# Feed-forward layers of a hybrid encoder: statistics inside the plain pair, a negation behind the last leading part, shared gate tiles, a third block begun early

## The chip, the cores and the metric

One NeuronCore of a Trainium2 chip runs the whole program as a single launch. The metric is the time of one execution on the device in microseconds; the number of a kernel is the median of its runs.

## What is computed

An encoder of width 1024 over 512 tokens with two layers. Each layer is a feed-forward network (FFN), a mixer (attention of several kinds), a cross attention to 256 memory rows, and a second FFN. So there are four FFNs, called FFN0 to FFN3 here. The change touches the FFNs, and the normalisation of the memory rows, which is prepared while FFN0 runs.

```python
def rmsnorm(x, g):
    y = xf * lax.rsqrt(jnp.mean(xf * xf, axis=-1, keepdims=True) + EPS)
    return (y * g.astype(jnp.float32)).astype(x.dtype)
def swiglu(x, wg, wu, wd):
    return (jax.nn.silu(x @ wg) * (x @ wu)) @ wd
...
    h = x
    for layer in range(DEPTH):
        h = h + 0.5 * swiglu(rmsnorm(h, g), wg, wu, wd)      # g, wg: [1024], [1024, 2816]
        h = h + even_mixer(...)                              # odd_mixer in layer 1
        h = h + memory_xattn(rmsnorm(h, mg), rmsnorm(mem, sg), wq, wkv, qg, kg, wo)
        h = h + 0.5 * swiglu(rmsnorm(h, g), wg, wu, wd)
```

## The kernel before

Activations lie transposed in SBUF, features on the partitions, as eight tiles of 128 by 512 tokens. Every fp32 operand of a product is split into a leading part (`xh`, `wh`, `hh`, rounded by ScalarE) and a rest (`xl`, `wl`, `hl`, a subtraction on VectorE), and a product is three matmuls: leading by leading, leading by rest, rest by leading (`LEAD` is the first two, `REST` the third). TensorE is called PE, VectorE DVE, ScalarE ACT, GpSimd POOL and SyncE SP.

An FFN has 22 blocks of 128 hidden features, taken in pairs. The first pair (`plain_pair`) multiplies the whole x with both blocks of wg and wu in plain matmuls of 128x512 (L317). The other ten pairs use a scheme with seven instead of eight products on quarters: `open_pair` (product of w11), `sum_pair` (products with the token sums t1 and t2, the second weight operand of which is the pair's `sh`/`sl` or `wh`/`wl`), `cross_pair` (products of w12 and with t3) and `close_pair` (`lower`, with t4, and `upper`). All of these matmuls are line L432. Weights of the quarters are read by SP (`fetch`, L419), two of them are sums that POOL makes with an accumulating DMA (L462, L484, the latter after ACT's negation at L483). `operand` (L410 on ACT, L411 on DVE) splits them; every third operand has tiles of its own (`sh`, `sl`, one buffer), the others share two buffers.

The norm of the tokens is not applied to x before the product but to the result: the factor R, one number for each token spread over 128 partitions, multiplies the gate's argument and the down result. Its way is: squares of x summed into `acc`; PE transposes `acc` (`column_sums`, L249); DVE reduces (L251) and forms v (L258); POOL raises v to the power -0.5 (L242, r); PE transposes r into a PSUM bank (L329); DVE copies it to R (L331). DVE also forms the token sums t1 to t4 (`token_sums`, tiles tq, L368 to L384) at this place.

After the pairs 4, 8 and 10 a chunk of hidden features (8, 8 and 6 blocks) is multiplied down (`down`, L553; the sum into x is L563 and L564). `down` has eight output blocks d. It begins two of them early without the chunk's last two hidden blocks (`down_products` with tail False) and brings these in when the gate of the last pair has made them (`hidden_parts`, L355 on ACT and L356 on DVE). In the last chunk the first block is begun before the last pair is closed, and the gates of that pair (L514 to L518) are computed in two halves, one behind `upper` and one behind `lower`.

PE executes in the order in which the code issues matmuls. The queues of the other engines are filled by a scheduler that follows priorities (`tc.high_priority`) and a constraint called `behind` (`issue_after`), which keeps an instruction from being queued before another one. The eight tiles of memory rows are loaded and squared in `mem_stats`, which the program calls behind pair 2 of FFN0; its column sums on PE stand ahead of the t1 product of pair 3.

Of the kernel before, what the change touches and what calls it, by code (L numbers as in the profile page):

```python
# [11 lines left out]
F32 = mybir.dt.float32  # L12
F32R = mybir.dt.float32r
BF = mybir.dt.bfloat16
AF = mybir.ActivationFunctionType
# [89 lines left out]
class Encoder:  # L105
# [45 lines left out]
    def wfill(self, tiles, src, sl, eng, after=None):  # L151
        nc = self.nc
        w, wh, wl = tiles
        dma = self.loaded = nc.sync.dma_start(w[:, sl], src[:, sl])
        nc.scalar.activation(wh[:, sl], w[:, sl], AF.Copy)  # L155
        with self.behind(after):
            eng.tensor_sub(wl[:, sl], w[:, sl], wh.bitcast(F32)[:, sl])  # L157
        return dma
# [104 lines left out]
    def ffn(self, pre):  # L263


        with ExitStack() as ctx:
            pool = lambda name: ctx.enter_context(self.tc.tile_pool(name=pre + name, bufs=1))
            f = self.f = SimpleNamespace(pre=pre, hp=pool("h"), tp=pool("t"), H={}, n=0, last=None)
            R = self.plain_pair()
            ends = [sum(CHUNKS[:c + 1]) // 2 for c in range(len(CHUNKS))]  # L270
            c = 0
            pair = self.open_pair(1)
            R()
            for p in range(1, FB // 2):
                final = p == FB // 2 - 1
                self.sum_pair(pair)
                if p in ends:
                    self.down(c)
                    c += 1
                self.cross_pair(pair)  # L280
                if final:
                    early = self.block(c, 0, True)
                    self.down_products(c, early, LEAD, False)
                    self.close_pair(pair, True)
                    self.down(c, early)
                else:
                    old, pair = pair, self.open_pair(p + 1)
                    self.close_pair(old, False)
                if p == 2 and self.mem_r is None:
                    self.mem_stats()  # L290

    def plain_pair(self):
        nc, I, f = self.nc, self.I, self.f
        xs, order = self.xs, self.order
        self.wshare = 0
        banks = []
        for b in range(2):
            ws, self.ws = self.ws, None
            after = self.rest if b == 0 and self.chained else None
            ws = ws or [self.wload(I[f.pre + w][b], 1024, after) for w in ("wg", "wu")]  # L300
            pp = [self.bank("pa"), self.bank("pb" if b else "pa")]
            banks.append(pp)
            if b == 0:
                head = order[:KB // 2]
                groups = [(ks, ((0, 0), (0, 1))) for ks in (head, order[KB // 2:KB - 1], order[KB - 1:])]
                if self.mem_r is None:
                    groups[1:1] = [(head, ((1, 0),))]
                    groups.append((order[KB // 2:], ((1, 0),)))
                else:
                    groups.append((order, ((1, 0),)))  # L310
            else:
                groups = [(order, ((0, 0), (0, 1), (1, 0)))]
            for ks, ops in groups:
                for w, p in zip(ws, pp):
                    for a, c in ops:
                        for k in ks:
                            nc.tensor.matmul(p, w[a][:, k * P:(k + 1) * P], xs[k][c],  # L317
                                             start=k == order[0] and a == c == 0, stop=k == order[-1] and a == 1)
        f.after = self.loaded
        with self.behind(self.summed), self.behind(self.squared):  # L320
            self.token_sums()
        v, r = self.stats(self.acc, QB)
        return lambda: self.plain_end(banks, r)

    def plain_end(self, banks, r):
        nc, f = self.nc, self.f
        p = self.bank("pb")
        for i in range(QB):
            nc.tensor.transpose(p[:, i * P:(i + 1) * P], r[:, i:i + 1].to_broadcast([P, P]), self.ident)  # L329
        f.R = f.tp.tile([P, S], F32, name="R", tag="R", bufs=1)  # L330
        nc.vector.tensor_copy(f.R, p)  # L331
        gs = f.tp.tile([P, 1024], F32, name="gs", tag="gs")
        for b in range(2):
            nc.vector.tensor_mul(gs[:, b * S:(b + 1) * S], banks[b][0], f.R)
        self.hidden(0, gs, [pp[1] for pp in banks])
# [66 lines left out]
    def operand(self, t, own=None):  # L402

        nc, f = self.nc, self.f
        if own is None:
# [4 lines left out]
        nc.scalar.activation(h, t, AF.Copy)  # L410
        nc.vector.tensor_sub(l, t, h.bitcast(F32))  # L411
        return h, l

# [2 lines left out]

    def fetch(self, t, p, q):
        with self.behind(self.f.after):
            self.nc.sync.dma_start(t, self.quarter(p, q))  # L419
        return t  # L420

    def raw_quarter(self, p, q):
# [48 lines left out]
    def cross_pair(self, pair):  # L471
# [8 lines left out]
        with self.tc.high_priority():  # L480
            s = f.tp.tile([P, 1024], F32, name="s3", tag="s3", bufs=2)
            self.fetch(s, p, 2)
            nc.scalar.activation(s, s, AF.Copy, scale=-1.0)  # L483
            nc.gpsimd.dma_start(s, self.quarter(p, 0), accum_op=OP.add)  # L484
            w = self.operand(s)
        self.product(pair.y, w, f.B["3"], False)
# [4 lines left out]
    def close_pair(self, pair, final):  # L491
# [16 lines left out]

        gu = pair.gu.rearrange("p (b z t) -> p b z t", b=2, z=2)
        if final:  # L510
            for b, step in enumerate((upper, lower)):
                step()
                gs = f.tp.tile([P, 1024], F32, name="gs", tag="gs")[:, :S]
                nc.vector.tensor_mul(gs, gu[:, b, 0, :], f.R)  # L514
                t = f.tp.tile([P, 1024], F32, name="t", tag="t")[:, :S]
                nc.scalar.activation(t, gs, AF.Tanh, scale=0.5)
                nc.vector.scalar_tensor_tensor(t, t, 1.0, gs, op0=OP.add, op1=OP.mult)  # L517
                nc.vector.tensor_mul(gs, t, gu[:, b, 1, :])  # L518
                self.hidden_parts(p, gs, b)
            return  # L520
        lower()
        upper()
# [33 lines left out]
    def down(self, c, first=None):  # L556
# [9 lines left out]
                self.made(d, self.x[d])  # L566

        early = [first or self.block(c, 0), self.block(c, 1)]
        for b in early[first is not None:]:
            self.down_products(c, b, LEAD, False)  # L570
        for b in early:
            self.down_products(c, b, REST, False)
        for d, b in enumerate(early):
            self.down_products(c, b, LEAD + REST, True)
            done(d, b[1])
        for d in range(2, KB):
            b = self.block(c, d)
            self.down_products(c, b, LEAD + REST, False)
            self.down_products(c, b, LEAD + REST, True)
# [506 lines left out]
    def mem_stats(self):  # L1086
        nc = self.nc
        with ExitStack() as ctx:
            mp = ctx.enter_context(self.tc.tile_pool(name="ms", bufs=2))
            acc, powed = None, self.powed  # L1090
            for k in range(KB):
                m = mp.tile([P, NMEM], F32, name="mem", tag="mem", bufs=4)
                with self.behind(self.loaded):
                    nc.sync.dma_start(m, self.I["memT"][k * P:(k + 1) * P, :])
                with self.behind(powed):
                    acc = self.square(acc, m, NMEM, mp)
            v, r = self.stats(acc, 2)
            self.mem_r = self.const.tile([P, 2], F32, name="mem_r")
# [420 lines left out]
```

## Time and profile before

| | us |
|---|---|
| three runs | 2183.46, 2184.88, 2185.17 |
| median | 2184.88 |
| the profiled execution | 2184.71 |
| its span in the trace | 2182.9 |

| engine | busy us | share of the span |
|---|---|---|
| PE | 2105.0 | 96% |
| DVE | 1571.6 | 72% |
| ACT | 1138.4 | 52% |
| POOL | 361.1 | 17% |

PE is busy for 2105.0 of the span of 2182.9 us, so all its idle time together is 77.9 us. Its busy time is not the same at all places: behind a long idle time the same matmuls take longer, which the granted clock of a stretch tells (1.00 is the level of 2.4 GHz, 0.50 that of 1.2 GHz). An idle time is charged to the instruction that came last by the trace.

### The profile page before, as it was taken

The numbers are of one execution on the slowest core, as the hardware profiler recorded it, in microseconds if no ns is written. First come the engines' busy times: TensorE is split into PE (matmuls) and PEld (weight loads), VectorE is DVE, ScalarE is ACT, GpSimd is POOL, SyncE is SP. The second block draws the span as 40 slices with busy tenths as digits, with TensorE's granted clock in tenths as the row PEclk, the third lists the DMA queues.
The fourth block names the chain that finished last, engine by engine and source line by source line (L and its number), as shares of the span: only waits on it lengthen the run. The fifth ranks groups of instructions, "written<-read, shape, count | busy, mean of one in ns | idle before, by whom it ended". The sixth has DMA issues, their size and how long they took to land. (4 is left out here: it accounts for less than half of the span.)

```text
span 2182.9 us, 32518 instructions
## 1 busy us (share of the span) xinstructions
PE 2105.0 (96%) x12834; PEld 1881.6 (86%) x12834; DVE 1571.6 (72%) x2242; ACT 1138.4 (52%) x1701; POOL 361.1 (17%) x319
## 2 busy tenths in 40 slices
PE   6999999999999989999999999999999998999998
PEld 5989997887778879898979899988888877989996
DVE  6858677479876687585778677675668677858675
ACT  5525444465686565363555355344778565525442
POOL 2100002335432110000020000003453022000000
PEclk8999999999999999999999999999999999999999
DMA  7637533322142166474346456334223215636532
GB/s 225 165 116 187 151 102 118 138 73 77 66 134 69 66 174 174 119 190 127 95 145 176 125 165 176 102 104 159 79 86 126 97 59 154 170 110 185 155 100 82
DMA packets 86121, 279.65 MB, mean 128 GB/s; under 512 B 9680, under 2 KB 12880, under 8 KB 85968
## 3 DMA queue, kind: packets, MB, share of 16 engines
q1 hardware_dynamic: 74448, 235.62, 32.6%
q0 software_dynamic: 11520, 41.95, 10.8%
q8 instruction: 101, 1.65, 0.3%
q14 instruction: 52, 0.43, 0.1%
HBM read 271.24 MB, written 6.29 MB: 127 GB/s over the span
## 5 line engine op out<-in xcount | busy, mean ns | idle before, releaser
L155 ACT ACTIVATE wh<-wf 128x1024 fp32r<-128x1024 f32 (+2 forms) x211 | 215.4, 1022 | 357.5 <-PE ps_pa L553 124.7
L157 DVE TENSOR_TENSOR wl<-wf,wh 128x1024 fp32r<-128x1024 f32 (+2 forms) x169 | 201.3, 1194 | 49.1 <-ACT wh L155 47.9
L411 DVE TENSOR_TENSOR wl<-s,wh 128x1024 fp32r<-128x1024 f32 x108 | 132.1, 1223 | 70.6 <-ACT wh L410 70.6
L410 ACT ACTIVATE wh<-s 128x1024 fp32r<-128x1024 f32 x108 | 114.3, 1058 | 105.7 <-PE ps_pb L432 38.2
L410 ACT ACTIVATE wh<-wf 128x1024 fp32r<-128x1024 f32 x84 | 89.1, 1060 | 107.8 <-PE ps_pa L553 31.2
L157 POOL TENSOR_TENSOR wl<-wf,wh 128x1024 fp32r<-128x1024 f32 x42 | 102.4, 2438 | 141.1 <-ACT wh L155 139.5
L484 POOL DMA_DIRECT2D s<-l_ffn_wq x40 | 35.4, 884 | 532.7 <-ACT s L483 532.7
L653 PE MATMUL ps_pa<-wh,xh 128*128 128x512 f32 x384 | 123.1, 402 | 0.0
L653 PE MATMUL ps_pa<-wh,xl 128*128 128x512 f32 x384 | 119.8, 393 | 0.0
L653 PE MATMUL ps_pa<-wl,xh 128*128 128x512 f32 x384 | 119.1, 391 | 0.0
L462 POOL DMA_DIRECT2D s<-l_ffn_wq x40 | 35.5, 887 | 448.5 <-DMA s<-l_ffn_wq 356.8
L411 DVE TENSOR_TENSOR wl<-wf,wh 128x1024 fp32r<-128x1024 f32 x84 | 102.8, 1224 | 4.4 <-ACT wh L410 4.4
L563 DVE TENSOR_TENSOR dn<-ps_pa,R 128x512 f32<-128x512 f32 x48 | 33.1, 690 | 95.9 <-PE ps_pa L553 95.9
L553 PE MATMUL ps_pb<-hh,wh 128*128 128x512 f32 x352 | 97.2, 394 | 0.0
L553 PE MATMUL ps_pb<-hl,wh 128*128 128x512 f32 x352 | 96.7, 393 | 0.0
L553 PE MATMUL ps_pb<-hh,wl 128*128 128x512 f32 x352 | 96.4, 392 | 0.0
L222 POOL TENSOR_TENSOR acc<-acc,sq 128x512 f32<-128x512 f32 (+1 forms) x37 | 46.6, 1260 | 268.1 <-ACT sq L221 267.1
L553 PE MATMUL ps_pa<-hh,wh 128*128 128x512 f32 x328 | 89.7, 392 | 0.0
L553 PE MATMUL ps_pa<-hh,wl 128*128 128x512 f32 x328 | 88.7, 389 | 0.0
L553 PE MATMUL ps_pa<-hl,wh 128*128 128x512 f32 x328 | 88.7, 389 | 0.0
L563 DVE TENSOR_TENSOR dn<-ps_pb,R 128x512 f32<-128x512 f32 x48 | 33.1, 689 | 76.2 <-PE ps_pb L553 76.2
L653 PEld LDWEIGHTS ps_pa<-wh,xl 128*128 128x128 f32 x384 | 72.6, 189 | 16.0
(376 smaller groups left out, 5997.3 us busy)
## 6 DMA issues: line engine op xcount, KB each, us to landing
wf<-l_ffn_wq SPq DMA_DIRECT2D x120, 512.0 KB, 3.3
s<-l_ffn_wq SPq DMA_DIRECT2D x80, 512.0 KB, 4.5
s<-l_ffn_wq POOLq DMA_DIRECT2D x80, 512.0 KB, 6.5
wf<-l_ffn_wd SPq DMA_DIRECT2D x64, 512.0 KB, 3.9
wf<-l_w_in SPq DMA_DIRECT2D x48, 512.0 KB, 3.2
wf<-l_ffn_wd SPq DMA_DIRECT2D x32, 384.0 KB, 3.1
wf<-l_mem_wkv SPq DMA_DIRECT2D x16, 512.0 KB, 3.3
wf<-l_w_out SPq DMA_DIRECT2D x16, 512.0 KB, 3.2
```

What stands on the lines that cost most here:

```text
L155: nc.scalar.activation(wh[:, sl], w[:, sl], AF.Copy)
L157: eng.tensor_sub(wl[:, sl], w[:, sl], wh.bitcast(F32)[:, sl])
L222: self.summed = (eng or nc.gpsimd).tensor_add(acc[:, :n], acc[:, :n], sq[:, :n])
L410: nc.scalar.activation(h, t, AF.Copy)
L411: nc.vector.tensor_sub(l, t, h.bitcast(F32))
L462: nc.gpsimd.dma_start(pair.s, self.quarter(p, 2), accum_op=OP.add)
L484: nc.gpsimd.dma_start(s, self.quarter(p, 0), accum_op=OP.add)
L553: self.nc.tensor.matmul(bank, w[a][:, j * P:(j + 1) * P], h, start=j == a == e == 0, stop=j == nb - 1 and (a, e) == ops[-1])
L563: nc.vector.tensor_mul(t, bank, f.R)
L653: nc.tensor.matmul(banks[i], xs[k][a][:, i * P:(i + 1) * P], w[b][:, kk * 512:kk * 512 + 512], start=k == a == b == 0, stop=k == KB - 1 an ...
```

## The change

It has five parts. (a) The transposes of `acc`, the reduction, v and r are issued inside the plain pair, behind the first product of its second block, at high priority, and the transposes of r with the copy to R follow right behind the plain pair, ahead of `open_pair(1)`. (b) The negation of ACT at the head of an FFN (L483) is queued behind the last leading part of the plain pair. (c) The two half gates of the last pair use the two halves of one `gs` and one `t` tile, and the parts of the first half are queued behind `lower`. (d) The first block of the last `down` does 12 instead of 8 matmuls ahead of `upper`, and a third block is begun early. (e) `fetch` records itself as the latest load, so that the loads and squares of the memory rows, which are queued behind the latest load and leading part, come later.

```diff
@@ wfill, operand, fetch
-        nc.scalar.activation(wh[:, sl], w[:, sl], AF.Copy)
+        self.leading = nc.scalar.activation(wh[:, sl], w[:, sl], AF.Copy)
...
-            self.nc.sync.dma_start(t, self.quarter(p, q))
+            self.loaded = self.nc.sync.dma_start(t, self.quarter(p, q))
@@ ffn, plain_pair
-            R = self.plain_pair()
+            self.plain_pair()
             pair = self.open_pair(1)
-            R()
...
+                    if b == 1 and p is pp[0]:
+                        with self.tc.high_priority():
+                            v, r = self.stats(self.acc, QB)
+        f.after, f.led = self.loaded, self.leading
...
-        v, r = self.stats(self.acc, QB)
-        return lambda: self.plain_end(banks, r)
         p = self.bank("pb")
         f.R = f.tp.tile([P, S], F32, name="R", tag="R", bufs=1)
-        nc.vector.tensor_copy(f.R, p)
+        with self.tc.high_priority():
+            for i in range(QB):
+                nc.tensor.transpose(p[:, i * P:(i + 1) * P], r[:, i:i + 1].to_broadcast([P, P]), self.ident)
+            nc.vector.tensor_copy(f.R, p)
@@ ffn, cross_pair
-                    self.down_products(c, early, LEAD, False)
+                    self.down_products(c, early, LEAD + REST, False)
...
-            nc.scalar.activation(s, s, AF.Copy, scale=-1.0)
+            with self.behind(f.led):
+                nc.scalar.activation(s, s, AF.Copy, scale=-1.0)
@@ close_pair
+            gs2 = f.tp.tile([P, 1024], F32, name="gs", tag="gs")
+            t2 = f.tp.tile([P, 1024], F32, name="t", tag="t")
+
+            def gate(b):
+                gs, t = (x[:, b * S:(b + 1) * S] for x in (gs2, t2))
                 nc.vector.tensor_mul(gs, gu[:, b, 0, :], f.R)
                 nc.scalar.activation(t, gs, AF.Tanh, scale=0.5)
                 nc.vector.scalar_tensor_tensor(t, t, 1.0, gs, op0=OP.add, op1=OP.mult)
                 nc.vector.tensor_mul(gs, t, gu[:, b, 1, :])
-                self.hidden_parts(p, gs, b)
+                return gs
+
+            upper()
+            with self.tc.high_priority():
+                gs = gate(0)
+            lower()
+            with self.tc.high_priority():
+                self.hidden_parts(p, gs, 0)
+                self.hidden_parts(p, gate(1), 1)
@@ down
+        if first is not None:
+            early.append(self.block(c, 2))
+        fresh = early[first is not None:]
+        for ops in (LEAD, REST):
+            for b in fresh:
+                self.down_products(c, b, ops, False)
...
-        for d in range(2, KB):
+        for d in range(len(early), KB):
@@ mem_stats
-                with self.behind(self.loaded):
+                with self.behind(loaded):
...
-                with self.behind(powed):
+                with self.behind(powed), self.behind(leading):
                     acc = self.square(acc, m, NMEM, mp)
```

Three places of the queues show what moves. The first is DVE at the head of FFN3 before the change; `s` and v are the statistics, `sl` is the rest of the second operand of pair 1.

```order
L377 SCALAR_TENSOR_TENSOR t1l<-tq,t1h 128x1024
L368 SCALAR_TENSOR_TENSOR tq<-x,cols,tq 128x256 x2
L375 TENSOR_TENSOR t3l<-tq,t3h 128x1024
L411 TENSOR_TENSOR wl<-wf,wh 128x1024
L375 TENSOR_TENSOR t2l<-tq,t2h 128x1024
L411 TENSOR_TENSOR wl<-s_17848,wh 128x1024
L251 TENSOR_REDUCE s<-ps_pb 128x4
L375 TENSOR_TENSOR t4l<-tq,t4h 128x1024
L466 TENSOR_TENSOR s_17848<-s_17848,wf 128x1024
L411 TENSOR_TENSOR wl<-wf,wh 128x1024
L258 TENSOR_SCALAR v<-s 128x4
L411 TENSOR_TENSOR sl<-s_17848,sh 128x1024
```

The same place of the same queue after the change, from the reduction on; lines have other numbers there (L366 is L368 of before, L375 is L377, L373 is L375, L409 is L411, L329 is L331).

```order
L251 TENSOR_REDUCE s<-ps_pb 128x4
L366 SCALAR_TENSOR_TENSOR tq<-x,cols,tq 128x256
L375 SCALAR_TENSOR_TENSOR t1l<-tq,t1h 128x1024
L366 SCALAR_TENSOR_TENSOR tq<-x,cols,tq 128x256 x2
L373 TENSOR_TENSOR t3l<-tq,t3h 128x1024
L258 TENSOR_SCALAR v<-s 128x4
L409 TENSOR_TENSOR wl<-wf,wh 128x1024
L373 TENSOR_TENSOR t2l<-tq,t2h 128x1024
L409 TENSOR_TENSOR wl<-s_17842,wh 128x1024
L373 TENSOR_TENSOR t4l<-tq,t4h 128x1024
L329 COPY R<-ps_pb 128x512
L464 TENSOR_TENSOR s_17842<-s_17842,wf 128x1024
```

The reduction has moved from behind five large operations to ahead of them, and v from behind eight to behind two; the copy to R now stands ahead of the operations that make `sl`, and behind these rows come `wl`, the two `gs` multiplications and then `sl`.

The second place is POOL in FFN0 before the change; `acc` are the sums of the memory squares, L462 and L484 the accumulating DMAs.

```order
L242 TENSOR_TENSOR r<-v,mhalf 128x4
L222 TENSOR_TENSOR acc<-acc,sq 128x256 x7
L484 DMA s_1009<-l_ffn_wq 128x1024
L462 DMA s_916<-l_ffn_wq 128x1024
L484 DMA s_1513<-l_ffn_wq 128x1024
L462 DMA s_1148<-l_ffn_wq 128x1024
L242 TENSOR_TENSOR r<-v,mhalf 128x2
```

And after the change (L483 and L460 are the accumulating DMAs there):

```order
L242 TENSOR_TENSOR r<-v,mhalf 128x4
L483 DMA s_1009<-l_ffn_wq 128x1024
L460 DMA s_916<-l_ffn_wq 128x1024
L483 DMA s_1513<-l_ffn_wq 128x1024
L222 TENSOR_TENSOR acc<-acc,sq 128x256 x6
L460 DMA s_1148<-l_ffn_wq 128x1024
L222 TENSOR_TENSOR acc<-acc,sq 128x256
L242 TENSOR_TENSOR r<-v,mhalf 128x2
```

The memory sums have moved behind three DMAs, and the last of them behind the DMA of `s_1148`, which belongs to pair 4. On ACT, in the same stretch, the negation of `s_489` now stands behind the last `wh` of the plain pair, and no memory square stands ahead of `t1h`; before, three did.

The third place is DVE at the last pair of FFN3, before the change, from the first half gate on.

```order
L514 TENSOR_TENSOR gs<-gu,R 128x512
L157 TENSOR_TENSOR wl<-wf,wh 128x768
L517 SCALAR_TENSOR_TENSOR t<-t,gs 128x512
L518 TENSOR_TENSOR gs<-t,gu 128x512
L356 TENSOR_TENSOR hl<-gs,hh 128x512
L514 TENSOR_TENSOR gs<-gu,R 128x512
L517 SCALAR_TENSOR_TENSOR t<-t,gs 128x512
L518 TENSOR_TENSOR gs<-t,gu 128x512
L356 TENSOR_TENSOR hl<-gs,hh 128x512
```

And after it:

```order
L515 TENSOR_TENSOR gs<-gu,R 128x512
L157 TENSOR_TENSOR wl<-wf,wh 128x768
L517 SCALAR_TENSOR_TENSOR t<-t,gs 128x512
L515 TENSOR_TENSOR gs<-gu,R 128x512
L518 TENSOR_TENSOR gs<-t,gu 128x512
L517 SCALAR_TENSOR_TENSOR t<-t,gs 128x512
L354 TENSOR_TENSOR hl<-gs,hh 128x512
L518 TENSOR_TENSOR gs<-t,gu 128x512
L354 TENSOR_TENSOR hl<-gs,hh 128x512
```

The first multiplication of the second gate has moved ahead of the last two operations of the first, and the two gates run interleaved.

## Rows read from the trace of the kernel before

**Rows 1.** What PE waited for: engine, line, releaser: us in total, times, longest

```profile
PE ps_pb L329 <- POOL r L242: 25.6, 4, 12.5
PE ps_pa L553 <- ACT hh L355: 14.9, 4, 3.7
PE ps_pb L432 <- DVE gu L489: 3.0, 4, 0.7
```

**Rows 2.** Timeline of PE at R in FFN0, FFN2, FFN3: start, us, [idle before]

```profile
48.80 1.11 PE L329 MATMUL ps_pb<-ident,r 128*128 128x128 f32 x4 [12.52 <-POOL r L242]
...
1152.70 0.65 PE L329 MATMUL ps_pb<-ident,r 128*128 128x128 f32 x4 [1.01 <-POOL r L242]
...
1850.25 1.11 PE L329 MATMUL ps_pb<-ident,r 128*128 128x128 f32 x4 [6.04 <-POOL r L242]
```

**Rows 3.** Timeline of PE in FFN3: first open product, t1, t2 by `sl`

```profile
1841.10 0.72 PE L432 MATMUL ps_pa<-xh,wh 128*128 128x256 f32 x4
...
1856.02 0.64 PE L432 MATMUL ps_pa<-t2h,sl 128*128 128x256 f32 x4
```

**Rows 4.** Timeline of DVE at the head of FFN3

```profile
1837.53 1.22 DVE L377 SCALAR_TENSOR_TENSOR t1l<-tq,t1h 128x1024 fp32r<-128x1024 f32 x1
...
1839.46 1.22 DVE L375 TENSOR_TENSOR t3l<-tq,t3h 128x1024 fp32r<-128x1024 f32 x1
...
1844.00 0.68 DVE L251 TENSOR_REDUCE s<-ps_pb 128x4 f32<-128x512 f32 x1
...
1848.08 1.22 DVE L411 TENSOR_TENSOR sl<-s,sh 128x1024 fp32r<-128x1024 f32 x1
...
1852.13 1.29 DVE L334 TENSOR_TENSOR gs<-ps_pa,R 128x512 f32<-128x512 f32 x2
```

**Rows 5.** Windows at r, FFN3, FFN2: PE PEld DVE ACT POOL busy, PEclk, DMA share

```profile
1848.20:1850.30 2.10, 0.05 (x1) 0.05 (x1) 2.07 (x2) 0.00 (x0) 1.95 (x1) 0.50 0.72 250
1151.60:1152.70 1.10, 0.09 (x1) 0.00 (x1) 0.36 (x1) 1.10 (x2) 1.04 (x1) 1.00 0.14 34
```

**Rows 6.** Timeline of FFN0: plain pair, memory square, t1h, t2 by `sl`

```profile
21.78 2.12 PE L317 MATMUL ps_pa<-xh,wh 128*128 128x512 f32 x8 [1.85 <-ACT wh L155]
...
35.41 0.42 ACT L221 ACTIVATE sq<-mem 128x256 f32<-128x256 f32 x1 [2.51 <-DMA mem<-memT]
35.73 1.04 ACT L372 ACTIVATE t1h<-tq 128x1024 fp32r<-128x1024 f32 x1
...
55.73 0.64 PE L432 MATMUL ps_pa<-t2h,sl 128*128 128x256 f32 x4
```

**Rows 7.** Timeline near the memory sums: SP's fetch, POOL's DMA, PE

```profile
85.83 0.33 SPq L419 DMA_DIRECT2D s<-l_ffn_wq  x1
...
91.14 0.86 POOL L462 DMA_DIRECT2D s<-l_ffn_wq  x1 [7.51 <-DMA s<-l_ffn_wq]
...
92.21 0.38 PE L249 MATMUL ps_pb<-ident,acc 128*128 128x128 f32 x2
```

**Rows 8.** Timeline of the end of FFN3: PE, ACT and DVE

```profile
2134.96 0.74 PE L432 MATMUL ps_pb<-xh,wh 128*128 128x256 f32 x4 [0.74 <-DVE gu L489]
...
2140.81 1.09 PE L553 MATMUL ps_pb<-hh,wh 128*128 128x512 f32 x4
...
2141.80 0.57 ACT L499 COPY gu<-ps_pa 128x512 f32<-128x512 f32 x1
...
2144.46 0.45 PE L553 MATMUL ps_pa<-hh,sh 128*128 128x512 f32 x1
...
2145.12 0.69 DVE L514 TENSOR_TENSOR gs<-gu,R 128x512 f32<-128x512 f32 x1
...
2148.64 0.80 PE L553 MATMUL ps_pa<-hh,sh 128*128 128x512 f32 x1 [3.73 <-ACT hh L355]
```

**Rows 9.** Windows behind that wait, first and last of the four FFNs

```profile
349.10:351.80 2.70, 2.70 (x8) 2.04 (x7) 0.83 (x2) 0.00 (x0) 0.00 (x0) 0.53 0.00 0
...
2149.20:2154.00 4.80, 4.80 (x13) 3.67 (x12) 1.75 (x4) 0.84 (x1) 0.00 (x0) 0.51 0.11 44
```

More of the change, by code (lines that the diff above doesn't have):

```diff
@@ L318, in plain_pair @@
                                              start=k == order[0] and a == c == 0, stop=k == order[-1] and a == 1)
-        f.after = self.loaded
+                    if b == 1 and p is pp[0]:
+                        with self.tc.high_priority():
+                            v, r = self.stats(self.acc, QB)
+        f.after, f.led = self.loaded, self.leading
         with self.behind(self.summed), self.behind(self.squared):
             self.token_sums()
-        v, r = self.stats(self.acc, QB)
-        return lambda: self.plain_end(banks, r)
-    def plain_end(self, banks, r):
-        nc, f = self.nc, self.f
         p = self.bank("pb")
-        for i in range(QB):
-            nc.tensor.transpose(p[:, i * P:(i + 1) * P], r[:, i:i + 1].to_broadcast([P, P]), self.ident)
         f.R = f.tp.tile([P, S], F32, name="R", tag="R", bufs=1)
-        nc.vector.tensor_copy(f.R, p)
+        with self.tc.high_priority():
+            for i in range(QB):
+                nc.tensor.transpose(p[:, i * P:(i + 1) * P], r[:, i:i + 1].to_broadcast([P, P]), self.ident)
+            nc.vector.tensor_copy(f.R, p)
         gs = f.tp.tile([P, 1024], F32, name="gs", tag="gs")
@@ L409, in operand @@
                 for n in (("sh", "sl") if own else ("wh", "wl"))]
-        nc.scalar.activation(h, t, AF.Copy)
+        self.leading = nc.scalar.activation(h, t, AF.Copy)
         nc.vector.tensor_sub(l, t, h.bitcast(F32))
@@ L510, in close_pair @@
         if final:
-            for b, step in enumerate((upper, lower)):
-                step()
-                gs = f.tp.tile([P, 1024], F32, name="gs", tag="gs")[:, :S]
+            gs2 = f.tp.tile([P, 1024], F32, name="gs", tag="gs")
+            t2 = f.tp.tile([P, 1024], F32, name="t", tag="t")
+            def gate(b):
+                gs, t = (x[:, b * S:(b + 1) * S] for x in (gs2, t2))
                 nc.vector.tensor_mul(gs, gu[:, b, 0, :], f.R)
-                t = f.tp.tile([P, 1024], F32, name="t", tag="t")[:, :S]
                 nc.scalar.activation(t, gs, AF.Tanh, scale=0.5)
@@ L568, in down @@
         early = [first or self.block(c, 0), self.block(c, 1)]
[L569 to L572, printed above, removed]
+        if first is not None:
[4 more added lines that the diff above has]
+                self.down_products(c, b, ops, False)
         for d, b in enumerate(early):
@@ L1089, in mem_stats @@
             mp = ctx.enter_context(self.tc.tile_pool(name="ms", bufs=2))
-            acc, powed = None, self.powed
+            acc, loaded, leading, powed = None, self.loaded, self.leading, self.powed
             for k in range(KB):
                 m = mp.tile([P, NMEM], F32, name="mem", tag="mem", bufs=4)
-                with self.behind(self.loaded):
+                with self.behind(loaded):
                     nc.sync.dma_start(m, self.I["memT"][k * P:(k + 1) * P, :])
-                with self.behind(powed):
+                with self.behind(powed), self.behind(leading):
                     acc = self.square(acc, m, NMEM, mp)
```

## The prediction

> **What bounds the kernel now.** The first thing to read is the list of engines, as in the table above: PE is busy for 2105.0 of 2182.9 us, so nothing that another engine does is worth anything unless PE waits for it, and all its idle time is 77.9 us. The second view is the list of what PE waited for [rows 1]. Three of its groups lie where the change works: 25.6 us before the transposes of r, once in each FFN, 14.9 us at the ends of the FFNs for `hh` of the last pair's second gate, and 3.0 us for the bank into which `upper` goes on. The timeline splits the first group into 12.52 us in FFN0, 1.01 in FFN2 and 6.04 in FFN3 [rows 2], which leaves 6.03 for FFN1. FFN0 has one more, 1.85 us, where PE waits for a `wh` that stands behind ACT's negation [rows 6]. That is 45.4 us of stalls. The third view is the granted clock: behind the 3.73-us stall at an FFN's end PE works 2.70 us at 0.53 in the first FFN and 4.80 us at 0.51 in the last, so 1.3 and 2.4 us are lost there [rows 9], 1.8 on average. With as much behind the longer stalls at three heads, some 58 us is all that can be won.
>
> **The ends of the FFNs (parts c and d).** In FFN3 `upper` starts at 2134.96 after 0.74 us of waiting, and the down block behind `lower` at 2140.81 [rows 8]. Between the two lie 48 matmuls that don't change. From 2140.81 PE does 16 down matmuls and begins the tail's first at 2144.46 [rows 8]: 3.65 us, 0.228 each. Four matmuls more in the first block are 0.91 us; they fill the 0.74, and the block behind `lower` starts at about 2141.0. There PE now has two fresh blocks, 24 matmuls or 5.5 us, where it had 12 and the four that moved: it comes to the tail at 2146.5 and to its second matmul at 2146.7.
>
> That one waits for the second gate, which before begins at 2145.12, although its `gu` was copied by 2141.80 + 0.57 = 2142.4 [rows 8]: DVE was still in the first gate, whose `hl` stands ahead of it. From 2145.12 to 2148.64 are 3.52 us, five steps of 0.70. With tiles of its own the second gate begins ahead of the first one's last multiplication, at about 2143.0, and the two run interleaved: on DVE `gs`, the first gate's `gs`, t, `hl` and `gs`, 0.69 each, with tanh beside them, and then `hh` on ACT, 0.63 by the same pitch. That is 4.1 us: 2147.1. So a stall of some 0.4 us stays, and PE is 1.54 us earlier with 12 matmuls (2.74 us) more done: 4.3 us for one FFN and 17.1 for four, whose stalls are alike (14.9 us in 4, the longest 3.7 [rows 1]). Behind the stall of 0.74 the clock did not fall (48 matmuls in the 5.85 us from 2134.96 to 2140.81 is 0.12 for one of 256 columns, as fast as 0.228 for 512), so behind 0.4 it should not either, and 1.8 us come back in each of four: 7.2. Sum for the ends 24.3. Bounds: if the gates did not interleave at all, 2148.64 would stay and only the 12 matmuls count, 11 us for four; nothing above 24.3 and four times 0.4, or 26. I take 24.3, because each step has a row.
>
> **The heads of FFN1 and FFN3 (part a).** In FFN3 the reduction runs at 1844.00, though PE was past its transposes by 1841.10 [rows 3], since DVE works through the token sums first [rows 4]. Its new place is ahead of `t1l`, which started at 1837.53; the reduction takes 0.68, so `t1l` moves to 1838.2, `t3l` follows after the same 1.93 us, and behind its 1.22 comes v at 1841.3. r takes 1.95 us beside a full DVE [rows 5]: 1843.4. PE, done with the plain pair by 1841.10, waits some 2.4 us instead of 6.04. Here the gain is not the stall that goes, since `sl` is late next. From `t3l` at 1839.46 to `sl` at 1848.08 DVE did seven large operations, the reduction and v (0.7 together) [rows 4], so a large one takes 1.14. Behind v now stand `wl`, t2l, `wl`, t4l (4.6), the copy to R (0.65, as one of the two `gs` [rows 4]), the subtraction and `wl` (2.3), two `gs` (1.3) and `sl` (1.2): 1851.4. PE starts the first matmuls with `sl` at 1856.02 before [rows 3]. After the change it has ahead of them the transposes (0.8), the open product (1841.10 to 1850.25 less 6.04, which is 3.1), the product with t1 (as much) and 0.96 of t2: from 1843.4 to about 1851. It waits up to 0.9 us for `sl` and goes on at 1851.4 to 1851.9. So 4.1 to 4.6 us are gained; I take 4.4 here and the same for FFN1, whose stall is the same: 8.8. Bounds for each: 0, if `sl` comes no sooner, and 7, the stall and a clock lost behind it.
>
> **The head of FFN2 (part a).** Its wait of 1.01 us [rows 2] goes: 1.0, between 0 and 1.
>
> **The head of FFN0 (parts a, b and e).** The negation goes behind the `wh` of the plain pair, and 1.85 us go. The three memory squares ahead of `t1h` go too: the last of them waited 2.51 us for its load and ran at 35.41, `t1h` at 35.73 [rows 6]. Without them `t1h` follows its sums, by my reading some 6 us sooner, v behind `t3l` comes at 34 to 35, and r two us later. PE arrives at 48.80 - 12.52 - 1.85 - 2.9 (the open product, now behind it), that is at 31.5, and waits about 5 us. The DVE steps of above then give `sl` at 44 to 46, where PE used it at 55.73 [rows 6]: 10 to 11.7 us. I take 10, since the operands of this head wait for loads as well. Bounds: 6 (the 1.85 and the 6 us of `t1h`, less two of clock), and 13.
>
> **The memory sums (part e): a new wait.** PE did them at 92.21 without waiting [rows 7]. Now their last addition on POOL stands behind the accumulating DMA of pair 4, which POOL issued only at 91.14, as it had waited for SP's fetch of 85.83 to land. PE and the fetch both move up by the 10 of above. In the times of before that DMA is issued by 92.0, and behind it come one addition (0.9, a row like the DMA's 0.86) and a semaphore or a late load, against PE at 92.2: between 0 and 5 us, of which I take 2.2. Queued on PE behind it is all of pair 3, whose operands have that time to get ready.
>
> An operation of POOL can be longer than its own work: r took 1.95 us where DVE was busy for 2.07 of 2.10 us, and 1.04 where it was busy for 0.36 of 1.10 [rows 5]. By the rows the addition is 0.9 us late at the worst, within my 2.2. The Trainium skill (SBUF — State Buffer, "Who interferes with whom") says that the only contention is an exclusive lock on the port pair that VectorE and GpSimd share, so the loser stands still until the other's instruction ends. The 0.9 us agree with its direction. By that rule the addition may wait for a whole operation of DVE, 1.22 us [rows 4], and the total would be 2144.0 instead of the sum below.
>
> **The sum.** 24.3 + 8.8 + 1.0 + 10 - 2.2 = 41.9 us. The profiled execution took 2184.71 us, 0.17 under the median, so the forecast is 2142.8 us.
>
> **Rivals.**
> - **The heads give little.** `sl`, not R, is what PE needs; if the steps ahead of it on DVE wait for ACT or a load, the stall moves from R to `sl` whole. For: DVE was busy for 2.07 of 2.10 us there [rows 5], and every operation still has to run. Against: 4 us of DVE's order ahead of `sl` is now done while PE is in its products. Then the 24.3 of the ends and some 3 of FFN0 are left: 2157.
> - **The ends give only the matmuls.** If the third block's operand or bank comes late, or the gates take turns as before, the ends give 11 instead of 24.3: 2156. For: the third block needs one weight buffer more at once. Against: before, the operand of the second block was ready early enough for PE to run 16 matmuls without a stall.
> - **The memory sums wait long.** The last addition hangs on a fetch, a landing and a square. Were it 10 us late, PE would lose 10 more: 2153.
> - **The clock at the heads.** Stalls of 2.4 and 5 us remain. If each cost 2 us of clock that no wait for `sl` hides, three of them give 2149.
> - **Slower than before.** One mechanism could do it: SP's memory loads hold up the fetches of pairs 3 and 4 behind them, because a load waits for a tile that a late square has to release, and PE waits for each operand. It decides from 42 us on, more than the two pairs between 55.73 and 92.21 take altogether [rows 6, 7]; 2190 if all of it came. For it speaks only that these loads now stand among the fetches.
>
> **How the numbers follow.** The forecast's own case (each part near its term) gets 0.57, with 2136 to 2149 as its range; heads that give little 0.15, ends that give only the matmuls 0.12, a long wait for the memory sums 0.08, the clock 0.06, slower 0.02. A measurement of this kernel can tell about 0.2%, or 4.4 us, from no change. All cases but the last are faster by more than that; two or three rivals together would come near no change, 0.02. So faster 0.96, same 0.02, slower 0.02. The range starts at 2133, where the heads come out some 8 us nearer to their upper bounds and the ends at theirs, and goes past the first two rivals: 2133 to 2159.
>
> **What the profile after would show.** Right: PE's waits for r come to some 10 us (5, 2.4, 0, 2.4) instead of 25.6, no wait for `hh` is above 1 us, no half clock lies behind the FFNs' ends, and there is a new wait for `sl` in each head and one of some 2 us before the memory sums. Wrong: a wait of 3 us or more for `hh`; one for the `wh` or the bank of the third block; v on DVE as late as before; `sl` of FFN3 less than 4 us sooner against the end of the plain pair.

## The result and the profile after

The changed kernel takes 2161.55 us (median of four runs, 2159.19 to 2162.37) against 2185.03 before; the ratio is 0.9891, with a 95% interval of 0.9874 to 0.9908. So it is faster by 23.5 us where 41.9 were forecast, and it lies above the range's end of 2159. The profiled execution took 2162.13 us with a span of 2160.3, 22.6 less than before.

The list of engines of the changed kernel, and below it what PE waited for (engine, line, releaser: us in total, times, longest):

```profile
PE 2101.7 (97%) x12830; PEld 1877.6 (87%) x12834; DVE 1575.2 (73%) x2242; ACT 1137.2 (53%) x1701; POOL 376.2 (17%) x319
```

```profile
PE ps_pb L328 <- POOL r L242: 18.4, 3, 7.5
...
PE ps_pb L249 <- POOL acc L222: 3.6, 1, 3.6
...
PE ps_pa L430 <- DVE sl L409: 1.3, 3, 0.5
...
PE ps_pa L561 <- ACT hh L353: 0.9, 4, 0.2
```

Against [rows 1] the wait for `hh` has gone from 14.9 to 0.9 us and the one for `gu` of `upper` is gone. But the wait for r has only gone from 25.6 to 18.4, where some 10 were forecast, and the memory sums have a new one of 3.6 us. POOL is busy for 15 us more with as many instructions, which is the first hint.

The end of FFN3 in the timeline of the changed kernel (start, us, instruction, idle before it), to be read against [rows 8]:

```profile
2118.93 0.74 PE L430 MATMUL ps_pb<-xh,wh 128*128 128x256 f32 x4
...
2124.78 1.09 PE L561 MATMUL ps_pb<-hh,wh 128*128 128x512 f32 x4
...
2126.86 0.69 DVE L515 TENSOR_TENSOR gs<-gu,R 128x512 f32<-128x512 f32 x1
...
2130.18 0.63 ACT L353 ACTIVATE hh<-gs 128x512 fp32r<-128x512 f32 x1 [1.36 <-DVE gs L518]
...
2130.86 0.50 PE L561 MATMUL ps_pa<-hh,sh 128*128 128x512 f32 x1 [0.23 <-ACT hh L353]
```

`upper` starts without a wait; the second gate starts 2.08 us behind the down block's first matmul, before it was 4.31 (2145.12 less 2140.81); PE waits 0.23 us for it instead of 3.73. The clock stays up behind that, as the windows of the changed kernel show for the first and the last FFN, with PEclk third from the end (before 0.53 and 0.51 [rows 9]):

```profile
349.00:352.00 3.00, 3.00 (x13) 2.50 (x14) 1.87 (x3) 1.04 (x2) 0.00 (x0) 1.00 0.00 0
2131.20:2136.00 4.80, 4.80 (x21) 3.68 (x20) 3.61 (x6) 1.70 (x2) 0.00 (x0) 1.00 0.14 55
```

From that down block on, FFN3's end gained 6.6 us: its start moved from 2140.81 to 2124.78, 16.0, the span shrank by 22.6. The terms said 4.3 + 1.8.

The head of FFN3 is where the forecast broke. The timeline of the changed kernel, DVE, POOL and PE together:

```profile
1824.96 0.17 DVE L258 TENSOR_SCALAR v<-s 128x4 f32<-128x4 f32 x1
1825.03 1.23 DVE L409 TENSOR_TENSOR wl<-wf,wh 128x1024 fp32r<-128x1024 f32 x1
1825.21 5.35 POOL L242 TENSOR_TENSOR r<-v,mhalf 128x4 f32<-128x4 f32 x1 [4.19 <-DVE v L258]
1826.16 1.23 DVE L373 TENSOR_TENSOR t2l<-tq,t2h 128x1024 fp32r<-128x1024 f32 x1
1827.30 1.23 DVE L409 TENSOR_TENSOR wl<-s,wh 128x1024 fp32r<-128x1024 f32 x1
1828.43 1.23 DVE L373 TENSOR_TENSOR t4l<-tq,t4h 128x1024 fp32r<-128x1024 f32 x1
1830.62 1.11 PE L328 MATMUL ps_pb<-ident,r 128*128 128x128 f32 x4 [5.44 <-POOL r L242]
1831.77 0.69 DVE L329 COPY R<-ps_pb 128x512 f32<-128x512 f32 x1 [2.11 <-PE ps_pb L328]
...
1839.88 0.39 PE L430 MATMUL ps_pa<-t2h,sl 128*128 128x256 f32 x1 [0.43 <-DVE sl L409]
```

v comes early, as planned: PE finished the plain pair at 1825.18 (1830.62 less 5.44), and v is done at 1825.13, just ahead of that. But r, which takes 1.04 us where DVE has room and took 1.95 in FFN3 before [rows 5], now takes 5.35. PE's t2 with `sl` came 16.1 us sooner than at 1856.02 [rows 3], and the end of the plain pair had already come 15.9 sooner (1841.10 against 1825.18): the head gained 0.2 us, not 4.4. FFN0 shows the same with r at 5.75 us, and behind it the late squares (ACT) and additions (POOL) of the memory rows, and the memory sums on PE:

```profile
35.59 5.75 POOL L242 TENSOR_TENSOR r<-v,mhalf 128x4 f32<-128x4 f32 x1 [4.81 <-DVE v L258]
...
39.21 1.23 DVE L464 TENSOR_TENSOR s<-s,wf 128x1024 f32<-128x1024 f32 x1
...
50.97 0.74 PE L430 MATMUL ps_pa<-t2h,sl 128*128 128x256 f32 x4 [0.48 <-DVE sl L409]
...
86.68 0.75 ACT L221 ACTIVATE sq<-mem 128x256 f32<-128x256 f32 x2 [3.29 <-DMA mem<-memT]
...
90.13 1.11 POOL L222 TENSOR_TENSOR acc<-acc,sq 128x256 f32<-128x256 f32 x1
...
91.30 0.69 PE L249 MATMUL ps_pb<-ident,acc 128*128 128x128 f32 x2 [3.60 <-POOL acc L222]
```

The head of FFN0 gained 4.8 us by t2 (55.73 [rows 6] to 50.97), not 10, and at the memory sums 0.9 are left of it (92.21 [rows 7] to 91.30). What came late there is a load of memory rows: ACT waits 3.29 us for it, and squares from 86.68 on. The DMA of pair 4, which stands ahead of POOL's last addition, costs no more than 0.6 us. The stretch behind the sums runs at the lower clock level of 1.2 GHz:

```profile
91.70:96.50 4.80, 4.80 (x25) 4.80 (x24) 3.29 (x4) 0.21 (x1) 0.00 (x0) 0.50 0.82 193
```

### The profile page after: what moved, and what is told of

Read it like the earlier page. It is cut to its first block, busy times and chain, and to the rows that moved or that the text cites. A ratio compares the mean times of both kernels' runs of the same rounds, so it can differ in the third digit from the quotient of the medians.

```text
span 2160.3 us, 32514 instructions
## 1 busy us (share of the span) xinstructions
PE 2101.7 (97%) x12830; PEld 1877.6 (87%) x12834; DVE 1575.2 (73%) x2242; ACT 1137.2 (53%) x1701; POOL 376.2 (17%) x319
## 4 chain that ended last, share of the span: by engine, by line
PE 86%; DVE 8%; ACT 2%; issue 1%; POOL 1%; DMA 1%; SPq 0%; DVEq 0%; POOLq 0%; ACTq 0%
PE ps_pa L430 26%; PE ps_pb L430 11%; PE ps_pa L663 10%; PE ps_pa L561 10%; PE ps_pb L561 9%; PE ps_pa L614 4%; PE ps_pa L316 2%; PE ps_pb L769 2%; PE ps_pa L1203 1%; PE ps_pb L821 1%; PE ps_pa L1060 1%; PE ps_pb L794 1%; DVE wl L157 1%; DVE xl L205 1%; PE ps_pa L979 1%
## 5 line engine op out<-in xcount | busy, mean ns | idle before, releaser
L409 DVE TENSOR_TENSOR wl<-s,wh 128x1024 fp32r<-128x1024 f32 x108 | 132.3, 1225 | 71.9 <-ACT wh L408 69.5
L483 POOL DMA_DIRECT2D s<-l_ffn_wq x40 | 35.6, 889 | 532.0 <-ACT s L482 532.0
L460 POOL DMA_DIRECT2D s<-l_ffn_wq x40 | 35.7, 891 | 463.7 <-DMA s<-l_ffn_wq 391.6
L409 DVE TENSOR_TENSOR wl<-wf,wh 128x1024 fp32r<-128x1024 f32 x84 | 102.8, 1224 | 12.9 <-ACT wh L408 12.8
L222 POOL TENSOR_TENSOR acc<-acc,sq 128x512 f32<-128x512 f32 (+1 forms) x37 | 52.2, 1411 | 251.9 <-ACT sq L221 250.8
L663 PEld LDWEIGHTS ps_pa<-wh,xl 128*128 128x128 f32 x384 | 72.7, 189 | 16.1
L663 PEld LDWEIGHTS ps_pa<-wl,xh 128*128 128x128 f32 x384 | 72.6, 189 | 16.0
```

Source lines behind the costliest of these rows:

```text
L222: self.summed = (eng or nc.gpsimd).tensor_add(acc[:, :n], acc[:, :n], sq[:, :n])
L460: nc.gpsimd.dma_start(pair.s, self.quarter(p, 2), accum_op=OP.add)
L663: nc.tensor.matmul(banks[i], xs[k][a][:, i * P:(i + 1) * P], w[b][:, kk * 512:kk * 512 + 512], start=k == a == b == 0, stop=k == KB - 1 an ...
```

## What holds r up

The rows already suggest a rule. In FFN3 DVE's row of four operations begins at 1825.03 and each starts some 0.1 us before the one ahead has ended; the row ends at 1828.43 + 1.23 = 1829.66, and r at 1825.21 + 5.35 = 1830.56, 0.90 later. In FFN0 the row ends at 39.21 + 1.23 = 40.44 and r at 41.34, 0.90 later. And in FFN3 of before r ended at 1850.20, 0.90 behind the end of `sl` at 1848.08 + 1.22 = 1849.30 [rows 4, 5]: the operation behind it there overwrites an input of `sl` and could not start before that. So the theory, called the **port theory** below: r can't read v as long as DVE runs operations with two SBUF inputs without a break, and needs 0.9 us from the break on. The rival: POOL is slow there for a reason of its own (its accumulating DMAs, the traffic), and the distance of 0.90 is chance. In the first four experiments DVE gets one operation more right behind v. The queues of POOL and of SP's loads stay as they are in all four. With the two operations of 128x512 the scheduler also puts some later operations of ACT and DVE at the heads in another order, the same for both, so these two kernels are to be compared with each other; with the two copies of 128x4 nothing else moves.

**A copy from PSUM, 128x512.** Its result is overwritten later; `self.vmade` is the operation that makes v.

```diff
-        nc.vector.tensor_scalar(v[:, :nb], s[:, :nb], 1.0 / D, EPS, op0=OP.mult, op1=OP.add)
+        self.vmade = nc.vector.tensor_scalar(v[:, :nb], s[:, :nb], 1.0 / D, EPS, op0=OP.mult, op1=OP.add)
...
                         with self.tc.high_priority():
                             v, r = self.stats(self.acc, QB)
+                            d = f.tp.tile([P, 1024], F32, name="gs", tag="gs")[:, :S]
+                            with self.behind(self.vmade):
+                                nc.vector.tensor_copy(d, banks[0][0])
```

> The changed kernel with one operation more on VectorE in each FFN, right behind v: a copy of a finished gate bank from PSUM to the gate tile, 128x512, whose result is overwritten later. It reads nothing from SBUF. Port theory: r on GpSimd can't read v while VectorE runs an unbroken row of operations with two SBUF inputs; this copy is a break in the row, so r takes 1.0 to 1.4 us instead of 5.75 (FFN0) and 5.35 (FFN1, FFN3), PE's wait for it falls from 5.4 to 1.0-1.6 us in FFN1 and FFN3 and from 7.5 to about 3 in FFN0, and the whole takes 2148 to 2152 us although there is more work. Rival (GpSimd is slow by itself there, or its DMAs and the traffic hold it): r stays at 5.3 us and the time is 2161 to 2164, since 0.6 us of VectorE work is added in each FFN.

Measured: 2148.47 us, ratio to before 0.9840 (0.9825 to 0.9855), 11 us less than the changed kernel by the two ratios to before (13 by the medians, which are of two series), with more work. The timeline of FFN3 in this kernel:

```profile
1812.75 0.17 DVE L258 TENSOR_SCALAR v<-s 128x4 f32<-128x4 f32 x1
1812.82 0.69 DVE L323 COPY gs<-ps_pa 128x512 f32<-128x512 f32 x1
1813.00 1.04 POOL L242 TENSOR_TENSOR r<-v,mhalf 128x4 f32<-128x4 f32 x1 [4.26 <-DVE v L258]
1813.42 1.22 DVE L412 TENSOR_TENSOR wl<-wf,wh 128x1024 fp32r<-128x1024 f32 x1
```

r takes 1.04 us in all four FFNs, though DVE is as full as before, and PE's waits for it come to 5.2 us instead of 18.4. A POOL that is slow by itself there is out, since its queue and the loads are the same.

**An addition of two SBUF tiles, 128x512, at the same place.**

```diff
-                                nc.vector.tensor_copy(d, banks[0][0])
+                                nc.vector.tensor_add(d, self.x[0], self.x[1])
```

> The same place and size, but the added operation is an addition of two SBUF tiles, 128x512. Port theory: the row of operations with two SBUF inputs is only longer, r takes 5.9 to 6.4 us in FFN1 and FFN3, the whole 2162 to 2166 us. Rival (any operation that stands between v and the next wl lets r through): r 1.0 to 1.4 us as with the copy from PSUM.

Measured in one execution: 2160.24 us. The timeline of FFN3:

```profile
1820.08 0.69 DVE L323 TENSOR_TENSOR gs<-x 128x512 f32<-128x512 f32 x1
1820.26 5.95 POOL L242 TENSOR_TENSOR r<-v,mhalf 128x4 f32<-128x4 f32 x1 [4.08 <-DVE v L258]
...
1824.09 1.22 DVE L376 TENSOR_TENSOR t4l<-tq,t4h 128x1024 fp32r<-128x1024 f32 x1
```

In FFN1 and FFN3 r takes 5.95 us, 0.60 more, the length that the row grew by, and ends at 1826.21, again 0.90 behind the end of t4l at 1825.31. So it is the kind of operation that counts, not that there is one: the two kernels differ in nothing else, and the one with the addition took 11.8 us more. The total was below the expectation since r took only 1.41 us in FFN0 and FFN2. In FFN2 nothing of DVE follows on the addition; in FFN0 a tq does:

```profile
35.49 0.68 DVE L323 TENSOR_TENSOR gs<-x 128x512 f32<-128x512 f32 x1
35.67 1.41 POOL L242 TENSOR_TENSOR r<-v,mhalf 128x4 f32<-128x4 f32 x1 [4.67 <-DVE v L258]
36.10 0.48 DVE L369 SCALAR_TENSOR_TENSOR tq<-x,cols,tq 128x256 f32<-128x256 f32 x1
```

r ends at 37.08, 0.91 behind the end of the addition at 36.17, so it got in between the addition and the tq. In FFN0 of the kernel with parts a and b alone, which follows below, it got in at such a place too, between t3l and a tq:

```profile
33.25 1.22 DVE L373 TENSOR_TENSOR t3l<-tq,t3h 128x1024 fp32r<-128x1024 f32 x1
33.42 1.95 POOL L242 TENSOR_TENSOR r<-v,mhalf 128x4 f32<-128x4 f32 x1 [6.45 <-DVE v L258]
34.38 0.48 DVE L366 SCALAR_TENSOR_TENSOR tq<-x,cols,tq 128x256 f32<-128x256 f32 x1
```

In FFN0 of the changed kernel, where r took 5.75 us, the tq is the first operation behind v, and four TENSOR_TENSOR follow on it. So a SCALAR_TENSOR_TENSOR behind a TENSOR_TENSOR was a break, here and in the kernel without part e (r 1.94 us), and a TENSOR_TENSOR behind a SCALAR_TENSOR_TENSOR was not; the reason is not shown.

Nor need the break read PSUM. Outside the FFNs of the changed kernel r also runs beside a reduction with one SBUF input, and takes 1.04 us:

```profile
1487.05 0.68 DVE L674 TENSOR_REDUCE ss<-sq 128x8 f32<-128x512 f32 x1
1487.22 1.04 POOL L242 TENSOR_TENSOR r<-v,mhalf 128x4 f32<-128x4 f32 x1 [16.86 <-DVE v L258]
```

**A copy from PSUM of 128x4.**

```diff
-                            d = f.tp.tile([P, 1024], F32, name="gs", tag="gs")[:, :S]
+                            d = self.small.tile([P, 4], F32, name="dum", tag="dum")
                             with self.behind(self.vmade):
-                                nc.vector.tensor_copy(d, banks[0][0])
+                                nc.vector.tensor_copy(d, banks[0][0][:, :4])
```

> The same place, but the copy from PSUM is 128x4, some 0.1 us. Port theory: it is over before GpSimd has v's signal (r began 0.1 to 0.25 us behind the start of v), so r stays near 5.3 us and the whole near 2161 us. If a break of any length is enough, r takes 1.0 to 1.4 us and the whole 2147 to 2151.

Measured in one execution: 2150.55 us, with r at 5.82 us in FFN0 and 5.42 in FFN1 and FFN3. So r behaved as the port theory says, and yet the total was some 10 us lower. Matmuls of 256 columns had become faster, in all parts of the FFNs; that is taken up again below. The same copy, written into the gate tile as the larger one was:

```diff
-                            d = self.small.tile([P, 4], F32, name="dum", tag="dum")
+                            d = f.tp.tile([P, 1024], F32, name="gs", tag="gs")[:, :4]
```

> The copy of 128x4 again, now written into the gate tile, so that no tile of its own moves the others in SBUF. With the tile of its own r took 5.82 and 5.42 us as expected, but the time was 2150.6, and the trace shows matmuls of 256 columns at 114 to 117 ns where all others have 120. If that came from where the tiles lie, the pitch is 120 again, r takes 5.3 to 5.8 us, and the time is 2160 to 2163 us. If a tiny operation helps in some way of its own: 2149 to 2152.

Measured: 2159.17 us (0.9871 to 0.9909 of before), r at 5.82 and 5.42 us. The port theory stands: a break that is over before POOL has its operand gives nothing.

## Which part of the change was worth what

**Parts c and d alone**, the kernel before with `close_pair`, `down` and the 12 matmuls of the change.

> The kernel before with parts c and d alone. If the terms of the ends were right (25 us against the terms' 24.3, of which 2 to 3 us are given back at the next stage) and the heads and part e together gave nothing, this takes 2160 to 2164 us, the time of the whole change. Rival (the heads do give 8 to 10 us and the ends correspondingly less): 2168 to 2172 us.

Measured: 2161.15 us, ratio 0.9893 (0.9875 to 0.9911), beside 0.9891 for the whole change. What PE waited for in this kernel:

```profile
PE ps_pb L329 <- POOL r L242: 25.7, 4, 12.2
...
PE ps_pa L562 <- ACT hh L355: 0.9, 4, 0.2
```

The whole gain is that of the ends; a, b and e together come to nothing that can be told from zero.

**Parts a and b alone**, the changed kernel with `close_pair`, `down`, the 8 matmuls, `fetch` and the memory squares of before.

> The kernel before with parts a and b alone. Port theory: r takes 5.35 us in FFN1 and FFN3 as in the whole change, so these two heads give less than 0.5 us each; FFN2 gives 1.0 to 1.9 us, and FFN0 some 8 to 10, since without part e nothing is lost at the memory sums: 2172 to 2176 us. By the forecast's terms (4.4 for each of FFN1 and FFN3, 1.0, 10) it would be 2163 to 2166.

Measured: 2179.70 us, ratio 0.9974 (0.9965 to 0.9984), 5.8 us less than before in that series, and less of a gain than I expected. What PE waited for in this kernel:

```profile
PE ps_pa L552 <- ACT hh L353: 14.9, 4, 3.7
PE ps_pb L328 <- POOL r L242: 13.4, 3, 5.4
...
PE ps_pa L430 <- ACT sh L408: 4.0, 1, 4.0
```

In FFN1 and FFN3 r takes 5.35 us as in the whole change. In FFN0 it takes 1.95, and a new wait of 4.0 us for `sh` has come: without part e the memory squares still stand in ACT's queue, now ahead of `sh`.

**The change without part e.**

```diff
-            self.loaded = self.nc.sync.dma_start(t, self.quarter(p, q))
+            self.nc.sync.dma_start(t, self.quarter(p, q))
...
-                with self.behind(powed), self.behind(leading):
+                with self.behind(powed):
```

> The changed kernel without part e: the memory rows' loads and squares are queued as before the change. If part e is what costs at the memory sums (3.60 us of waiting and 2.4 us of half clock behind it), these go and the whole takes 2155 to 2157 us. Rival: part e pays for itself, since without it the memory squares stand ahead of t1h on ACT again; then v and R of FFN0 come some 5 us later and the time is 2160 to 2163 us.

Measured: 2154.31 us, ratio 0.9868 (0.9851 to 0.9884). That is 5 us less than the changed kernel by the ratios (7 by the medians). The wait at the memory sums is gone, but not all of it is its doing: another order of DVE came with the edit, and r of FFN0 takes 1.94 us in it instead of 5.75. Against the runs of before beside each, parts c and d gained 24.4 us, a and b 5.8, and this kernel, which has the four, 28.7. So a and b do bring something, and part e takes it back. In the other direction the trace has the wait for `sh` again:

```profile
45.19 1.02 PE L430 MATMUL ps_pa<-t2h,sh 128*128 128x256 f32 x4 [2.52 <-ACT sh L408]
```

**The copy of 128x512 behind v, and no part e.**

> The changed kernel with the copy of 128x512 from PSUM behind v and without part e, both at once. If the two repairs work at different places of the program, r takes 1.04 us in the four FFNs, PE does not wait at the memory sums, and the time is that with the copy less the 2.4 us of waiting and 1.2 us of clock left there: 2144 to 2146 us. Rival (FFN0 gets the same time back from either, since both end at the same sl): 2147 to 2150.

Measured: 2149.90 us, ratio 0.9843 (0.9826 to 0.9860), not less than the 0.9840 with the copy alone. The time is the rival's: FFN0 gets it back once. With r at 1.04 us, PE waits 2.74 us for `sh` there, and not at all in the kernel with the copy and part e. So part e does pay at the head of FFN0, and takes it back at the memory sums.

**The copy, and the memory sums one pair later on PE**, loads and squares as in the change.

```diff
                 if p == 2 and self.mem_r is None:
-                    self.mem_stats()
+                    sums = self.mem_stats()
+                    next(sums)
+                if p == 3 and sums:
+                    next(sums, None)
...
+            yield
             v, r = self.stats(acc, 2)
```

> The changed kernel with the copy of 128x512 from PSUM behind v, and with PE's memory sums behind pair 3 instead of pair 2, loads and squares as in the changed kernel. If the sums' wait was only that PE asked too early, the 2.4 us of waiting and 1.2 us of half clock go and nothing takes their place: 2144 to 2146 us. Rival (loads and squares that stand late hold up what follows them on SP, ACT and GpSimd, so that PE waits for an operand of pair 4 instead): 2147 to 2150.

Measured: 2144.79 us, ratio 0.9829 (0.9813 to 0.9844). No wait is left at the memory sums and none took its place in pairs 3 and 4, so PE had merely asked too early. The largest waits of this kernel:

```profile
PE ps_pa L319 <- ACT wh L155: 8.8, 4, 7.7
PE ps_pb L800 <- DVE e L927: 7.0, 8, 2.9
PE ps_pb L334 <- POOL r L242: 5.0, 3, 2.8
```

With r read at once and the sums late, the gain is 37.6 us over the runs of before beside it (2182.35), 4.3 short of the 41.9 forecast for the change, and by other terms: the 2.2 us at the memory sums are not lost, the head of FFN0 gains 12.3 us by t2 (it starts at 43.48 instead of 55.73) and not 10, and the heads of FFN1 and FFN3 give less than forecast, as the next section shows.

**An unused tile.** The changed kernel with 128x4 taken in SBUF and not used; every engine's queue is the same as without it.

```diff
                             v, r = self.stats(self.acc, QB)
+                            self.small.tile([P, 4], F32, name="dum", tag="dum")
```

> The changed kernel with one tile of 128x4 that nothing uses, 32 bytes a partition with its two buffers, ahead of most other tiles in SBUF. Every queue is as in the changed kernel. If matmuls of 256 columns run at 114 to 117 ns because of where the tiles lie, this takes 2149 to 2153 us with r at 5.35 us as before; if the faster matmuls of the earlier run were a chance of that execution, 2160 to 2163 and 120 ns.

Measured: 2150.21 us, ratio 0.9850 (0.9835 to 0.9866), with r at 5.75 and 5.35 us. PE's matmuls by form in the changed kernel (line, output and operands, tile, count | busy, mean ns | idle before):

```profile
L561 PE MATMUL ps_pb<-hh,wl 128*128 128x512 f32 x352 | 95.4, 389 | 0.0
L430 PE MATMUL ps_pa<-t2l,wh 128*128 128x256 f32 x192 | 30.9, 283 | 0.0
```

and in that with the unused tile:

```profile
L562 PE MATMUL ps_pb<-hh,wl 128*128 128x512 f32 x352 | 96.4, 392 | 0.0
L431 PE MATMUL ps_pa<-t2l,wh 128*128 128x256 f32 x192 | 29.6, 276 | 0.0
```

The kernel before with the same tile:

> The kernel before the change with the same unused tile. If the placement is a thing of its own that has nothing to do with the change, it gains here what it gains there: 2173 to 2177 us, and matmuls of 256 columns at 114 to 117 ns. Otherwise 2183 to 2187.

Measured: 2175.28 us, ratio 0.9960 (0.9945 to 0.9975), 7 us less than the runs of before beside it, with the same 276 ns. So this has nothing to do with the change. And the version with both repairs and the tile:

> The same with the unused tile of 32 bytes: if both hold, 2133 to 2137 us, r at 1.04 us, no wait at the memory sums, and matmuls of 256 columns at 114 to 117 ns.

Measured: 2133.77 us (2132.33 to 2137.49), ratio 0.9780 (0.9764 to 0.9797). It beats both kernels.

## Why the prediction was wrong

**The ends: right.** The forecast had 24.3 us; FFN3's end gained 6.6 against 6.1 of the terms, and parts c and d alone gave the whole 23 to 24. The interleaved gates left 0.23 us of `hh` wait where 0.4 was forecast, the clock stayed up, and `upper` starts unhindered.

**The heads of FFN1 and FFN3: the step that failed.** The prediction said "r takes 1.95 us beside a full DVE". It took 5.35. The 1.95 was read from a row of before in which DVE was just as busy, so the price looked like one for a full DVE; it was the price of the distance to the next break in DVE's row (0.03 us between `sl` and the operation that overwrites its input) plus 0.90. In the new order v is followed by four operations with two SBUF inputs that don't depend on each other, and then by the copy to R, which itself waits for r: there is no break until DVE has run out of work. The step ahead of r (v in FFN3 level with PE's arrival) held. 8.8 us were forecast for the two heads; FFN3's rows show 0.2. What a prompt r is worth there, the kernel with the copy from PSUM shows, in FFN3:

```profile
1814.09 0.65 PE L331 MATMUL ps_pb<-ident,r 128*128 128x128 f32 x4 [1.13 <-POOL r L242]
...
1822.11 0.74 PE L433 MATMUL ps_pa<-t2h,sh 128*128 128x256 f32 x4 [1.62 <-ACT sh L411]
...
1824.43 1.22 PE L433 MATMUL ps_pa<-t2h,sl 128*128 128x256 f32 x4 [1.11 <-DVE sl L412]
```

From the end of the plain pair to t2 by `sl` PE needs 11.5 us here (1824.43 less 1812.96, where its wait of 1.13 begins), 14.7 in the changed kernel, 14.9 before, and 16.8 in the kernel with the addition. So r is worth 5.3 us at this head where nothing else differs, but the head gains only 3.4 over before: in the order that came with the copy, ACT makes a `wh` ahead of `sh`, PE waits for `sh` and then for `sl`, and the granted clock is 0.50 behind that, from 1824.40 to 1827.30. The steps that the forecast had behind r, with up to 0.9 us of wait for `sl` and none for `sh`, were thus not shown in its own order. Of the 11 to 13 us that the copy took off the changed kernel, some 8 lie in FFN0, 3 in FFN1 and 2 in FFN3, and none in FFN2.

**The rule weighed in the prediction** from the Trainium skill (SBUF — State Buffer, "Who interferes with whom") agrees in kind, since DVE's operations are what held r up. I applied it to the memory additions, took the wait for one instruction of DVE, and put the difference at 1.2 us. The runs show that the loser doesn't get in at the end of one instruction: r stood still through four or five of them, 5.35 and 5.95 us. They show which operations of DVE hold r up, and not the lock itself.

**The head of FFN0: half.** By t2 it gained 4.8 of 10 us. r again took 5.75 instead of 1.95. With r at 1.04, in the kernel with the copy from PSUM, that t2 starts at 44.11, 11.6 us sooner than before, so the rest of the term held.

**The memory sums: a wait as forecast, its size and its cause off.** 2.2 us were forecast; 3.60 of waiting came, and behind it the lower clock, which the term left out: 4.80 us at 0.50, another 2.4. The last addition is queued behind the DMA of pair 4, as forecast, but that cost no more than 0.6 us; what came late was a load of memory rows (3.29 us of ACT's waiting, until 86.68), which the term named without a price.

**FFN2: right**, its wait of 1.01 us is gone.

Of the 18 to 19 us between the forecast and the measurement, twice FFN3's 4.2 lie in FFN1 and FFN3, 5.2 in FFN0's head (10 less 4.8) and 3.8 at the memory sums (3.60 and 2.4 less 2.2). That is 17.4. The ends and FFN2's head gave about 2 us more than their terms, and the stretches between the FFNs' ends and the next heads gave about 3 back: the matmul at 1104.70 of before, at the end of FFN1, starts 9.5 us sooner in the changed kernel, and the one at 1142.78, in the plain pair of FFN2, only 8.4. Why they do is not shown. The rival "the heads give little" was the one that came true, by another mechanism than its own, and together with a larger wait at the memory sums; its time of 2157 had left no room for that, nor had the range.

## What to carry to other kernels

Where GpSimd makes a small result that others wait for, look at what VectorE has in its queue right behind the operand: if these are operations on two SBUF tiles that don't depend on each other, GpSimd got its operand in these runs when the row ended, not one instruction later, and moving the operand earlier gained nothing. An operation that reads PSUM, put there, was such a break, even a useless one: 0.69 us of VectorE work in each FFN took 11 us off. And a price that is read from one row holds for the neighbours of that row; before it is used elsewhere, see what ended the wait in it.

## What the runs showed that was not expected

32 bytes a partition in SBUF that nothing uses made the matmul of 256 columns shorter, from 283 to 276 ns for t2 by the leading weights, and the one of 512 slightly longer (389 to 392 for `hh` by the rest), with every queue the same. These times overlap; from start to start the median went from 120 to 118 ns and from 227 to 229. The whole gained 9 us in the changed kernel by the ratios, 7 in the one before and 11 in the one with both repairs. So two kernels that differ in what they allocate can differ by up to 0.5% for that alone, and an experiment that needs a scratch tile should take it from one that is there already. Which tile's place it is, and what about the place matters, was not tried.
